# Attention scores on 64 array rows, rotary step with its half swap made by transfers, and a by-class copy of u, in a hybrid decoder block on one core

## The chip, the cores and the metric

The kernel runs on one core of one Trainium2 chip. The metric is device time in microseconds (us), as the median of several runs; a smaller number is better. Beside the timed runs, one execution was taken by the hardware profiler; all times of single instructions below come from that one execution.

## The reference, cut to what matters

One decoder layer on 512 tokens and 1024 features, all in float32: a SwiGLU feed-forward, a token-mixing part, a second feed-forward, a final norm. The change is nearly all in the token mixing. For normed and modulated tokens `u` it computes

```
proj = u @ w_in                      # pool p | q | k | v | gates
q, k = rope(q), rope(k)              # t1*cos - t2*sin , t2*cos + t1*sin  on the two 32-wide halves of a head
group 0: 4 heads, each query sees the last 128 keys
group 1: 4 heads, every 4th token; group 2: 4 heads, every 16th token
s = q k^T / 8, masked; softmax; o = p v       # head size 64
y_attn = sum over groups, weighted by their softmax denominators
y_pool = pooled p (windows 2, 4, 8, 16) through small matrices
out = (gate_p * (y_pool @ w_pb) + gate_a * (y_attn @ w_ab)) @ w_out
```

Groups 1 and 2 are computed on the four residue classes of the token number modulo 4 (class c holds the tokens 4i + c).

## The kernel before, in words

**Products.** Every float32 weight is split into two float32r parts (`whi`, `wlo`) and every activation likewise (`UH`, `UL` for u), and each product is three matmuls. TensorE runs these in an order written out by hand, nearly without a gap. Weights come in chunks of 512 KB into three buffers (`raw`); ScalarE makes `whi` (L298), VectorE makes `wlo` (L310) into a ring of seven chunks. `look`, `take`, `split` and `fetch` keep that pipeline some three chunks ahead of the matmuls. Each engine works its own program strictly in order; SyncE (queue SP) issues the transfers in program order as well.

**The mixing stage** (`mix`, L1173) goes so:

1. `head` makes q and k of group 0 in four banks, in the last 22 us before 381 us of the span.
2. `rope` (L974) turns two banks (first halves of four heads, second halves of four heads; `lay_mix` has ordered the columns so, by `qk_cols`) into `qt` or `kt`. Four VectorE products with cos and sin (L981), then two subtractions and two additions on 64 rows each (L987, L988). For groups 1 and 2 it also reorders the tokens by class, so that L987 and L988 read with a step of four elements.
3. The values of group 0 (L1222 to L1224), in four token blocks of 24 matmuls with 256 columns.
4. Eight tiles (`mm_tile`, L990; 24 matmuls with 512 columns each) make q and k of groups 1 and 2, and two more the pool inputs. Between their matmuls, hooks at given places k = 0..7 of a tile put the attention of group 0: one unit (token block n, pair of heads hp) per tile. A unit passes through `at_prep` (L1010: VectorE makes `qz`, a copy of q with the rows of the other head zeroed by the mask `hmask`), `at_scores` (L1022: fp32 matmuls with all 128 rows, then masking, maximum and exponentials), one tile later `at_turn` (L1062: transposes through TensorE, copy by ScalarE), and another tile later `at_values` (L1079).
5. `pool_diff` (L1140) works on GpSimd with the scratch tiles rt0 to rt2.
6. The values of groups 1 and 2 (L1272 to L1274): four classes c of 24 matmuls with 512 columns each. The stationary operand is `UH[k][:, c::4]` or `UL[k][:, c::4]`, read with a step of four elements. The units of groups 1 and 2, two per class, are hooked in here, their scores at k = 5 and k = 6.
7. Gates, merge and the output product follow.

**The second feed-forward** (`ffn2`, L787) makes the block sums for its saved products in a list of steps (`u_steps`, L673): additions on VectorE (L679, L695) and splits (L685 on ScalarE, then L686 on VectorE), put between the first tiles.

Of the kernel before, what the change touches and what calls it, by code (L numbers as in the profile page):

```python
# [14 lines left out]
P = 128  # L15
# [121 lines left out]
class Kernel:  # L137
# [535 lines left out]
    def u_steps(self, n):  # L673

        nc, v = self.nc, self.nc.vector
        (a11, a12), (a21, a22) = self.U4

        def add(o, x, y, op):
            return lambda: v.tensor_tensor(o, x, y, op=op)  # L679

        def split(i, u):
            def f():
                hi, lo = self.S[i]
                if i < 3:
                    nc.scalar.activation(hi, u, AF.Copy)  # L685
                    v.tensor_tensor(lo, u, hi, op=OP.subtract)  # L686
                    return
                nc.scalar.activation(hi, u.rearrange("p (k t) -> p k t", k=4), AF.Copy)
                v.tensor_tensor(lo, u.rearrange("p (k t) -> p k t", k=4), hi, op=OP.subtract)
            return f  # L690
# [96 lines left out]
    def ffn2(self):  # L787
        self.put, self.now = [], 0
        bk = [self.nb() for _ in range(4)]
        self.head(2, bk, AF.Silu)  # L790
        adds, (s2, s1, s0, last) = self.u_steps(2)
        self.todo = adds[:3] + [s0, adds[3], s2, adds[4], s1, adds[5]]
        do = lambda n: [self.todo.pop(0)() for _ in range(n)]
        for j in range(2):
            self.ffn_post(j, self.ffn_silu(j, bk[2 * j]), bk[2 * j + 1])
            do(2 + j)
# [4 lines left out]
        self.ffn(2, 4, last)  # L801
# [172 lines left out]
    def rope(self, pa, pb, dst, classes=1):  # L974

        v = self.nc.vector
        t = [self.rt.tile([P, 528], F32, name=f"rt{i}")[:, :T] for i in range(4)]
        for o, x, y in ((t[0], pa, self.cos), (t[1], pb, self.sin), (t[2], pb, self.cos), (t[3], pa, self.sin)):  # L980
            v.tensor_tensor(o, x, y, op=OP.mult)  # L981
        for half in (0, 1):
            rows = slice(64 * half, 64 * half + 64)
            cols = slice(T * half, T * half + T)
            src = [x[rows].rearrange("p (i c) -> p c i", c=classes) for x in t]
            to = [dst[r, cols].rearrange("p (c i) -> p c i", c=classes) for r in (slice(0, 64), slice(64, 128))]
            v.tensor_tensor(to[0], src[0], src[1], op=OP.subtract)  # L987
            v.tensor_tensor(to[1], src[2], src[3], op=OP.add)  # L988
# [21 lines left out]
    def at_prep(self, u):  # L1010

        kind, n, hp = u
        gs, toks = self.at_tokens(u)
        qz = self.aw.tile([P, T], F32, name="qz")
        for i, g in enumerate(gs):
            q = self.qt[g][:, hp * T:hp * T + T]
            for h in range(2):
                self.nc.vector.tensor_scalar(qz[:, (2 * i + h) * P:(2 * i + h + 1) * P], q[:, toks],
                                             self.hmask[:, h:h + 1], None, op0=OP.mult)
        self.qz[u] = qz  # L1020

    def at_scores(self, u):  # L1022
        kind, n, hp = u
        nc = self.nc
        M = nc.tensor.matmul
        self.si ^= 1
        S = self.bS[self.si]
        qz = self.qz.pop(u)
        gs, toks = self.at_tokens(u)
        for h in range(2):  # L1030
            o = h * 256
            if kind == 0:
                k = self.kt[0][:, hp * T:hp * T + T]
                if n == 0:
                    M(S[:, o + P:o + 2 * P], qz[:, h * P:h * P + P], k[:, 0:P], start=True, stop=True)
                else:
                    M(S[:, o:o + 2 * P], qz[:, h * P:h * P + P], k[:, (n - 1) * P:(n + 1) * P], start=True, stop=True)
            else:
                for i, g in enumerate(gs):
                    k = self.kt[g][:, hp * T:hp * T + T]  # L1040
                    M(S[:, o + i * P:o + i * P + P], qz[:, (2 * i + h) * P:(2 * i + h + 1) * P], k[:, toks],
                      start=True, stop=True)
# [8 lines left out]
        for h in range(2):  # L1051
            cs = slice(h * 256 + c0, h * 256 + 256)
            nc.vector.tensor_tensor_reduce(p[:, cs], S[:, cs], mask[:, c0:], 1.0, 3.0 * NEG, op0=OP.add, op1=OP.max,
# [25 lines left out]
    def at_values(self, u):  # L1079
# [14 lines left out]
        if kind == 0:  # L1094
            self.nc.vector.tensor_copy(self.o1[:, n, P * hp:P * hp + P], O)
        elif hp == 1:
            self.nc.vector.tensor_copy(self.o23[:, n, :256], self.bO[:, :256])
# [42 lines left out]
    def pool_diff(self, t, bank):  # L1140
# [3 lines left out]
        p, a, b = (self.rt.tile([P, 528], F32, name=f"rt{i}") for i in range(3))  # L1144
# [28 lines left out]
    def mix(self):  # L1173
        nc, tc = self.nc, self.tc
        v, M = nc.vector, nc.tensor.matmul
        self.prob, self.probT, self.pd, self.qz = {}, {}, {}, {}
        self.si = self.ti = 0
# [4 lines left out]
        with tc.tile_pool(name="ma", bufs=1) as ma, tc.tile_pool(name="rt", bufs=1) as self.rt, \  # L1182
                tc.tile_pool(name="aw", bufs=2) as self.aw, tc.tile_pool(name="stp", bufs=1) as self.stp:
# [17 lines left out]
            self.rope(bk[0], bk[1], self.qt[0])  # L1201
            self.rope(bk[2], bk[3], self.kt[0])
# [9 lines left out]
            for n in range(4):  # L1212
# [3 lines left out]
                if n == 3:  # L1216
                    self.at_prep((0, 0, 0))
# [7 lines left out]
                nc.scalar.activation(self.v1[:, n, :], b[:, :256], AF.Copy)  # L1225
            self.held = None
# [5 lines left out]
            def hooks(new, extra=(), nxt=()):  # L1232
# [6 lines left out]
                for i, u in enumerate(new):  # L1239
                    if u not in self.qz:  # L1240
                        h.setdefault(i, []).insert(0, lambda u=u: self.at_prep(u))
                    h.setdefault(5 + i, []).append(lambda u=u: self.at_scores(u))
                for u in nxt:
                    h.setdefault(6 + len(new) - 1, []).append(lambda u=u: self.at_prep(u))
# [14 lines left out]
            b = self.mm_tile(hooks([], nxt=g23[0]))  # L1259
            self.pool_diff(0, b)  # L1260
            b = self.mm_tile(hooks(g23[0], nxt=g23[1]))
# [3 lines left out]
            for c in range(4):  # L1265
                hk = hooks(g23[c + 1] if c < 3 else [])
                b = self.nb()
                for k in range(KT):
                    for f in hk.get(k, ()):
                        f()  # L1270
                    hi, lo = w[k]
                    M(b, self.UH[k][:, c::4], hi, start=k == 0, stop=False)  # L1272
                    M(b, self.UH[k][:, c::4], lo, start=False, stop=False)  # L1273
                    M(b, self.UL[k][:, c::4], hi, start=False, stop=k == KT - 1)  # L1274
# [73 lines left out]
    def build(self):  # L1348
# [24 lines left out]
        self.invf, self.hmask, self.icnt, self.ident = cst[:, 0:1], cst[:, 1:3], cst[:, 3:35], cst[:, 35:163]  # L1373
# [144 lines left out]
def constants():  # L1518
    i = np.arange(P)
    invf = (ROPE_THETA ** (-np.arange(0, HEAD_DIM, 2) / HEAD_DIM)).astype(np.float32)  # L1520
    hm = np.stack([(i % 64 // 32 == h) for h in range(2)], axis=1).astype(np.float32)
# [8 lines left out]
    return np.concatenate([invf[i % 32][:, None], hm, cnt, np.eye(P, dtype=np.float32),  # L1530
# [43 lines left out]
```

## Time and profile before

| what | value |
|---|---|
| time, median of 3 runs | 1013.88 us (1013.68 to 1016.19) |
| the profiled execution's own time | 1014.89 us |
| its span in the trace | 1013.1 us |
| TensorE busy | 1004.4 us, 99% of the span |
| VectorE busy | 763.9 us, 75% |
| ScalarE busy | 442.8 us, 44% |
| GpSimd busy | 26.9 us, 3% |
| mean granted TensorE clock | 0.999 |

The profiled execution's own time lies 1.8 us over its span: what is outside the first and the last instruction. A busy TensorE is one with a matmul somewhere in its pipe; one matmul of 512 columns is shown with some 0.39 us, while the next starts 0.23 us after it, so the pace has to be read from starts, not from durations. "PEld" is the loading of the stationary operand, which runs beside the matmul before.

### The profile page before, as it was taken

To read this page: it belongs to the slowest core of one execution; us is meant where nothing else is said; L and a number is where in the kernel's file an instruction comes from. 1 tells how busy PE (TensorE), PEld (TensorE's weight loads), DVE (VectorE), ACT (ScalarE), POOL (GpSimd) and SP (SyncE) were. 2 spreads that over 40 slices of the span, in tenths; PEclk is the share of its full clock that TensorE was granted. 3 is DMA by queue.
4 is the path that set the end of the run, shared out by engine and by line. 5 is a ranking of instruction groups with operands and counts; after the bars stand their busy time and mean duration, and the time that the engine had idled before them with its cause. 6 is when DMAs were issued, how large, how long until landed. Compare 5 with 4: busy or idle time off the path is not lost.

```text
span 1013.1 us, 15788 instructions
## 1 busy us (share of the span) xinstructions
PE 1004.4 (99%) x6460; PEld 912.8 (90%) x6460; DVE 763.9 (75%) x1117; ACT 442.8 (44%) x674; POOL 26.9 (3%) x31
## 2 busy tenths in 40 slices
PE   9999999999999999999999999999999999999997
PEld 7888999989899999889988888998899899998997
DVE  7989979789797677878447776577787776676754
ACT  6443644525435443334424323454365255352553
POOL 0000000000000000008000000000000000000002
PEclk9999999999999999999999999999999999999999
DMA  9755456455454323122155773412344234241312
GB/s 338 274 202 209 146 160 221 149 173 169 152 182 136 104 77 104 61 65 84 32 199 177 257 270 107 125 56 69 88 167 125 81 105 146 84 137 51 100 47 83
DMA packets 43146, 139.61 MB, mean 138 GB/s; under 512 B 4929, under 2 KB 8257, under 8 KB 43074
## 3 DMA queue, kind: packets, MB, share of 16 engines
q1 hardware_dynamic: 42498, 138.08, 41.4%
q8 instruction: 50, 0.82, 0.3%
q10 hardware_dynamic: 576, 0.52, 0.2%
q14 instruction: 22, 0.18, 0.0%
HBM read 135.82 MB, written 2.77 MB: 137 GB/s over the span
## 4 chain that ended last, share of the span: by engine, by line
PE 87%; DVE 7%; issue 2%; DMA 2%; ACT 1%; POOL 0%; SPq 0%; POOLq 0%; DVEq 0%; ACTq 0%
PE bank L342 15%; PE bank L343 15%; PE bank L341 15%; PE bank L719 10%; PE bank L721 10%; PE bank L720 10%; DVE wlo L310 2%; PE bank L1501 1%; PE bank L1503 1%; PE bank L1505 1%; PE bank L1093 1%; PE bank L1272 1%; DVE H L864 1%; PE bank L1273 1%; PE bank L1274 1%
## 5 line engine op out<-in xcount | busy, mean ns | idle before, releaser
L310 DVE TENSOR_TENSOR wlo<-raw,whi 128x1024 fp32r<-128x1024 f32 (+6 forms) x166 | 174.3, 1061 | 66.0 <-ACT whi L298 65.7
L298 ACT ACTIVATE whi<-raw 128x1024 fp32r<-128x1024 f32 (+6 forms) x166 | 149.9, 920 | 49.2 <-DVE raw L242 41.5
L719 PE MATMUL bank<-UH,whi 128*128 128x256 f32 x544 | 150.6, 277 | 0.2 <-ACT u L726 0.2
L721 PE MATMUL bank<-UH,wlo 128*128 128x256 f32 x544 | 150.5, 277 | 0.0
L720 PE MATMUL bank<-UL,whi 128*128 128x256 f32 x544 | 150.5, 277 | 0.0
L341 PE MATMUL bank<-HI,whi 128*128 128x512 f32 (+1 forms) x406 | 146.6, 361 | 0.0
L342 PE MATMUL bank<-HK,whi 128*128 128x512 f32 (+1 forms) x406 | 146.4, 361 | 0.0
L343 PE MATMUL bank<-HI,wlo 128*128 128x512 f32 (+1 forms) x406 | 146.2, 360 | 0.0
L341 PE MATMUL bank<-UH,whi 128*128 128x512 f32 (+1 forms) x400 | 145.9, 365 | 0.0
L343 PE MATMUL bank<-UH,wlo 128*128 128x512 f32 (+1 forms) x400 | 141.8, 355 | 0.5 <-DVE wlo L310 0.5
L342 PE MATMUL bank<-UL,whi 128*128 128x512 f32 (+1 forms) x400 | 141.8, 355 | 0.1
L310 DVE TENSOR_TENSOR wlo<-X,whi 128x1024 fp32r<-128x1024 f32 (+4 forms) x106 | 111.7, 1063 | 33.4 <-ACT whi L298 33.0
L298 ACT ACTIVATE whi<-X 128x1024 fp32r<-128x1024 f32 (+4 forms) x106 | 95.7, 926 | 47.8 <-DVE X L242 47.0
L719 PE MATMUL bank<-SH,whi 128*128 128x256 f32 x408 | 113.8, 279 | 0.1
L720 PE MATMUL bank<-SL,whi 128*128 128x256 f32 x408 | 113.6, 278 | 0.0
L721 PE MATMUL bank<-SH,wlo 128*128 128x256 f32 x408 | 113.6, 278 | 0.0
L719 PEld LDWEIGHTS bank<-UH,whi 128*128 128x128 f32 x544 | 102.1, 188 | 0.7 <-ACT u L726 0.4
L720 PEld LDWEIGHTS bank<-UL,whi 128*128 128x128 f32 x544 | 102.4, 188 | 0.3
L721 PEld LDWEIGHTS bank<-UH,wlo 128*128 128x128 f32 x544 | 102.1, 188 | 0.0
L342 PEld LDWEIGHTS bank<-HK,whi 128*128 128x128 f32 x406 | 76.3, 188 | 11.8 <-DVE HK L647 0.4
L341 PEld LDWEIGHTS bank<-HI,whi 128*128 128x128 f32 x406 | 76.5, 188 | 11.5
L343 PEld LDWEIGHTS bank<-HI,wlo 128*128 128x128 f32 x406 | 76.4, 188 | 11.6
(227 smaller groups left out, 1761.1 us busy)
## 6 DMA issues: line engine op xcount, KB each, us to landing
ada<-wada SPq DMA_DIRECT2D x47, 512.0 KB, 5.2
raw<-wmix SPq DMA_DIRECT2D x44, 512.0 KB, 3.7
raw<-wf1i SPq DMA_DIRECT2D x32, 512.0 KB, 4.3
raw<-wf2i SPq DMA_DIRECT2D x30, 512.0 KB, 3.5
X<-wf2i SPq DMA_DIRECT2D x14, 512.0 KB, 3.5
cs<-wada SPq DMA_DIRECT2D x12, 512.0 KB, 3.5
AR<-wada SPq DMA_DIRECT2D x12, 512.0 KB, 4.3
raw<-wf2o SPq DMA_DIRECT2D x12, 512.0 KB, 3.5
```

What stands on the lines that cost most here:

```text
L298: self.nc.scalar.activation(self.hi[:, y], r[:, x], AF.Copy)
L310: self.nc.vector.tensor_tensor(self.lo[:, y], r[:, x], self.hi[:, y], op=OP.subtract)
L341: M(ps, hi, uh, start=start, stop=False)
L342: M(ps, hi, ul, start=False, stop=False)
L343: M(ps, lo, uh, start=False, stop=stop)
L719: M(o, hi, uh, start=start and p == 0 and k == 0, stop=False, skip_group_check=True)
L720: M(o, hi, ul, start=False, stop=False, skip_group_check=True)
L721: M(o, lo, uh, start=False, stop=k == 3, skip_group_check=True)
L864: v.scalar_tensor_tensor(self.H[m + i], b, gate[:, m + i:m + i + 1], self.H[m + i], op0=OP.mult, op1=OP.add)
L1093: M(o, pt[:, blk * P:blk * P + P], v, start=i == 0, stop=i == len(srcs) - 1)
L1272: M(b, self.UH[k][:, c::4], hi, start=k == 0, stop=False)
L1273: M(b, self.UH[k][:, c::4], lo, start=False, stop=False)
```

## The change

Five things change.

1. **Layout of q and k.** A bank now holds two whole heads (64 rows each) and not four half heads; `qk_cols` is gone. `rope` becomes two steps. `rope_a`, right behind the bank: ScalarE copies the bank times +1 or -1 (`sign`) to a scratch tile, four transfers on SP swap the 32-row halves of it into a second tile `w`, and VectorE writes bank * cos into `dst`. `rope_b`, later: VectorE multiplies `w` by sin in place and adds it to `dst`. For group 0, `rope_b` stands between the blocks of its values; for the others at k = 6 of the next tile.
2. **Scores.** `at_prep`, `qz` and `hmask` are gone. The scores of head 0 use rows 0 to 63, those of head 1 rows 64 to 127, of `qt` and `kt` directly, each head into a bank of its own.
3. **Places.** The two units of a token block are hooked into one tile (both scores at k = 5, both `at_exp` behind them), the next tile has no new unit. In the class loop both units of a class have their scores at k = 5.
4. **By class.** `by_class` copies u's tokens 4i + c side by side (ScalarE, 16 copies of 128x512), half a class at a time into two buffers of each kind, and the matmuls of the values of groups 2 and 3 (in the code's count from 0: 1 and 2) take these as their stationary operand.
5. **Block sums.** In `ffn2` a split is put into the list as two steps, so that an addition of VectorE stands between ScalarE's copy and VectorE's subtraction.

The scratch tile rt0 becomes a part of `tr`. The copy of group 0's result out of its bank is made once for two units. The diff, cut:

```diff
-def qk_cols(base, g, second):
-    return np.concatenate([base + (4 * g + h) * 64 + 32 * second + np.arange(32) for h in range(4)])
...
-            for s in (0, 1):
-                ch.append(_fmajor(w_in, qk_cols(base, g, s)))
+            for hp in (0, 1):
+                ch.append(_fmajor(w_in, base + (4 * g + 2 * hp) * 64 + np.arange(P)))
...
+            x = u if i < 3 else u.rearrange("p (k t) -> p k t", k=4)
+            parts = [lambda: nc.scalar.activation(self.S[i][0], x, AF.Copy),
+                     lambda: v.tensor_tensor(self.S[i][1], x, self.S[i][0], op=OP.subtract)]
+            return parts if n else lambda: [f() for f in parts]
...
-        self.todo = adds[:3] + [s0, adds[3], s2, adds[4], s1, adds[5]]
+        self.todo = adds[:3] + [s0[0], adds[3], s0[1], s2[0], adds[4], s2[1], s1[0], adds[5], s1[1]]
...
-    def rope(self, pa, pb, dst, classes=1):
...
+    def rope_a(self, bank, dst, hp, classes, t, w):
+        nc = self.nc
+        nc.scalar.activation(t, bank, AF.Copy, scale=self.sign)
+        for i in range(4):
+            o = i ^ 1
+            nc.sync.dma_start(w[32 * o:32 * o + 32], t[32 * i:32 * i + 32])
+        by = lambda x: x.rearrange("p (i c) -> p c i", c=classes)
+        nc.vector.tensor_tensor(dst[:, hp * T:hp * T + T].rearrange("p (c i) -> p c i", c=classes), by(bank), by(self.cos),
+                                op=OP.mult)
+
+    def rope_b(self, dst, hp, classes, w):
         v = self.nc.vector
...
+        d = dst[:, hp * T:hp * T + T].rearrange("p (c i) -> p c i", c=classes)
+        v.tensor_tensor(w, w, self.sin, op=OP.mult)
+        v.tensor_tensor(d, d, w.rearrange("p (i c) -> p c i", c=classes), op=OP.add)
...
-    def at_prep(self, u):
...
     def at_scores(self, u):
...
+        for i, g in enumerate(gs):
+            for h in range(2):
+                rows = slice(64 * h, 64 * h + 64)
+                q, k = (x[g][rows, hp * T:hp * T + T] for x in (self.qt, self.kt))
+                if kind:
+                    o, ks = slice(i * P, i * P + P), toks
                 else:
...
+                    o, ks = (slice(0, 2 * P), slice((n - 1) * P, (n + 1) * P)) if n else (slice(P, 2 * P), toks)
+                S = self.bS[h][:, 2 * P * hp:2 * P * hp + 2 * P]
+                nc.tensor.matmul(S[:, o], q[:, toks], k[:, ks], start=True, stop=True, skip_group_check=True)
...
+            for i in range(4):
+                self.rope_a(bk[i], *to[i], 1, self.v23[:, i, :], sw[i])
...
+                for i in ((), (0, 1), (2,), (3,))[n]:
+                    self.rope_b(*to[i], 1, sw[i])
...
+                h.setdefault(5, []).extend(lambda f=f, u=u: f(u) for f in (self.at_scores, self.at_exp) for u in new)
...
-            todo = [[(0, n, hp)] for n in range(4) for hp in range(2)]
+            todo = [x for n in range(4) for x in ([(0, n, hp) for hp in range(2)], [])]
+            rest = []
             for g in (1, 2):
                 for dst in (self.qt[g], self.kt[g]):
-                    ps = [self.mm_tile(hooks(todo.pop(0), nxt=todo[0] if todo else ())) for s in range(2)]
-                    self.rope(ps[0], ps[1], dst, 4)
+                    for hp in range(2):
+                        b = self.mm_tile(hooks(todo.pop(0), rest))
+                        rt = [self.scratch(2 * i + hp)[:, :T] for i in range(2)]
+                        self.rope_a(b, dst, hp, 4, *rt)
...
+                        rest = [(6, lambda dst=dst, hp=hp, w=rt[1]: self.rope_b(dst, hp, 4, w))]
...
+            def by_class(i):
...
+                c, k = i // 2, i % 2 * 4
+                uc[i] = [self.uw.tile([P, T], F32R, name=n) for n in ("uch", "ucl")]
+                for o, x in zip(uc[i], (self.UHv, self.ULv)):
+                    nc.scalar.activation(o.rearrange("p (k i) -> p k i", k=4),
+                                         x.rearrange("p (k i c) -> p c k i", k=KT, c=4)[:, c, k:k + 4], AF.Copy)
...
+            b = self.mm_tile(hooks(g23[0], [(1, lambda: by_class(0)), (2, lambda: by_class(1))]))
...
-                    M(b, self.UH[k][:, c::4], hi, start=k == 0, stop=False)
-                    M(b, self.UH[k][:, c::4], lo, start=False, stop=False)
-                    M(b, self.UL[k][:, c::4], hi, start=False, stop=k == KT - 1)
+                    (hi, lo), (uh, ul) = w[k], (x[:, k % 4 * P:k % 4 * P + P] for x in uc[2 * c + k // 4])
+                    M(b, uh, hi, start=k == 0, stop=False)
+                    M(b, uh, lo, start=False, stop=False)
+                    M(b, ul, hi, start=False, stop=k == KT - 1)
+                    if k % 4 == 3 and c < 3:
+                        by_class(2 * c + 2 + k // 4)
```

More of the change, by code (lines that the diff above doesn't have):

```diff
@@ L800, in ffn2 @@
         self.ffn_pair(3)
-        self.ffn(2, 4, last)
+        self.ffn(2, 4, lambda: [f() for f in last])
     def open_ffn(self):
@@ L972, in trig_spread, with scratch @@
             self.nc.sync.dma_start(self.cs[32 * b:32 * b + 32], self.scr2)
-    def rope(self, pa, pb, dst, classes=1):
-        v = self.nc.vector
[L979 to L988, printed above, removed]
+    def scratch(self, i):
+        return self.rt.tile([P, 528], F32, name=f"rt{i}") if i else self.tr[:, :528]
+    def rope_a(self, bank, dst, hp, classes, t, w):
[8 more added lines that the diff above has]
+    def rope_b(self, dst, hp, classes, w):
+        v = self.nc.vector
+        d = dst[:, hp * T:hp * T + T].rearrange("p (c i) -> p c i", c=classes)
+        v.tensor_tensor(w, w, self.sin, op=OP.mult)
+        v.tensor_tensor(d, d, w.rearrange("p (i c) -> p c i", c=classes), op=OP.add)
     def mm_tile(self, hooks=()):
@@ L1024, in at_scores, with at_exp @@
         nc = self.nc
[L1025 to L1028, printed above, removed]
         gs, toks = self.at_tokens(u)
[L1030 to L1035, printed above, removed]
-                else:
[L1037 to L1042, printed above, removed]
+        for i, g in enumerate(gs):
[4 more added lines that the diff above has]
+                    o, ks = slice(i * P, i * P + P), toks
+                else:
+                    o, ks = (slice(0, 2 * P), slice((n - 1) * P, (n + 1) * P)) if n else (slice(P, 2 * P), toks)
+                S = self.bS[h][:, 2 * P * hp:2 * P * hp + 2 * P]
+                nc.tensor.matmul(S[:, o], q[:, toks], k[:, ks], start=True, stop=True, skip_group_check=True)
+    def at_exp(self, u):
+        kind, n, hp = u
+        nc = self.nc
         p = self.aw.tile([P, T], F32, name="prob")
@@ L1143, in pool_diff @@
         w0 = POOL_W[2 * t]
-        p, a, b = (self.rt.tile([P, 528], F32, name=f"rt{i}") for i in range(3))
+        p, a, b = (self.scratch(i) for i in range(3))
         d = self.kt[0][:, T * t:T * t + T]
@@ L1175, in mix @@
         v, M = nc.vector, nc.tensor.matmul
-        self.prob, self.probT, self.pd, self.qz = {}, {}, {}, {}
-        self.si = self.ti = 0
+        self.prob, self.probT, self.pd = {}, {}, {}
+        self.ti = 0
         outer = ExitStack()
@@ L1520, in constants @@
     invf = (ROPE_THETA ** (-np.arange(0, HEAD_DIM, 2) / HEAD_DIM)).astype(np.float32)
-    hm = np.stack([(i % 64 // 32 == h) for h in range(2)], axis=1).astype(np.float32)
+    sign = np.where(i % 64 < 32, 1, -1).astype(np.float32)
     cnt = np.zeros((P, 32), np.float32)
```

56 lines of the change are left out of this document (15 added, 41 removed).

## The prediction

> **What bounds the kernel now.** I read the page's busy times first, then the waits of TensorE, then the stretches of the mixing stage.
>
> ```profile
> span 1013.1 us, 15788 instructions
> PE 1004.4 (99%) x6460; PEld 912.8 (90%) x6460; DVE 763.9 (75%) x1117; ACT 442.8 (44%) x674; POOL 26.9 (3%) x31
> ```
>
> TensorE has work in it for all but 8.7 us. So an edit pays only if it takes matmul time away, quickens the pace, or ends one of TensorE's few waits. Its waits, first for 380 to 531 us of the span, then for 660 to 720 us, are one each:
>
> ```profile
> PE bank L1070 <- ACT prob L1058: 0.2, 1, 0.2
> PE bank L343 <- DVE wlo L310: 0.5, 1, 0.5
> ```
>
> 0.7 us in all. Then the windows, with the columns PE, PEld, DVE, ACT, POOL: everything from the first tile behind group 0's values to the last values of the classes, and the class loop alone.
>
> ```profile
> 393.10:504.50 111.40, 111.10 (x599) 98.72 (x598) 79.27 (x193) 42.09 (x103) 21.56 (x20) 1.00 0.25 79
> 466.20:504.50 38.30, 38.30 (x226) 37.50 (x226) 21.35 (x65) 18.03 (x46) 14.46 (x14) 1.00 0.17 53
> ```
>
> Granted clock 1.00; VectorE and ScalarE have room. The edit must shorten these 111.4 us. All its savings are TensorE's.
>
> **By-class copies.** Starts in TensorE's timeline give the pace: twelve matmuls of the class loop, then twelve plain ones.
>
> ```profile
> 474.24 0.40 PE L1272 MATMUL bank<-whi,UH 128*128 128x512 f32 x1
> ...
> 476.82 0.39 PE L1274 MATMUL bank<-whi,UL 128*128 128x512 f32 x1
> ...
> 504.46 0.40 PE L341 MATMUL bank<-UH,whi 128*128 128x512 f32 x1
> ...
> 506.96 0.39 PE L343 MATMUL bank<-UH,wlo 128*128 128x512 f32 x1
> ```
>
> Eleven steps take 2.58 us (0.2345 each) with the operand read in steps of four, 2.50 us (0.2273) without. 96 matmuls: 0.69 us. The loads say why:
>
> ```profile
> L1272 PEld LDWEIGHTS bank<-whi,UH x32: 307/309/311, 465.9 to 503.5; 128*128 128x128 f32 x32
> L1222 PEld LDWEIGHTS bank<-whi,UH x32: 188/192/192, 381.5 to 392.6; 128*128 128x128 f32 x32
> ```
>
> A stepped load lasts 0.31 us against 0.19. Small matmuls put between cannot cover it. Scores in a plain tile, then in the loop:
>
> ```profile
> 463.87 1.05 PE L1041 MATMUL bank<-k,qz 128*128 128x128 f32 x8
> 464.68 0.48 PE L341 MATMUL bank<-UH,whi 128*128 128x512 f32 x1
> 465.00 0.39 PE L342 MATMUL bank<-UL,whi 128*128 128x512 f32 x1
> ...
> 470.80 1.05 PE L1041 MATMUL bank<-k,qz 128*128 128x128 f32 x8
> 471.61 0.60 PE L1272 MATMUL bank<-whi,UH 128*128 128x512 f32 x1
> 472.05 0.40 PE L1273 MATMUL bank<-wlo,UH 128*128 128x512 f32 x1
> ```
>
> The first big matmul behind an interruption takes 0.32 us (0.093 over pace) in a plain tile and 0.44 (0.205 over) in the loop. The loop has 14 interruptions (4, 4, 4, 2 by class); with both scores at k = 5 it has 11 (3, 3, 3, 2). 14 x 0.205 - 11 x 0.093 = 1.85 us. Together **2.5 us**.
>
> **Fewer places.** In the eight tiles and the first pool tile group 0 has 24 interruptions (scores, turn, values, each 8); two units at a time leave 4 + 8 + 4. The second pool tile goes from two to one. 9 x 0.093 = **0.8 us**.
>
> **Scores on half the rows.** From the chain of waits, four records of 256 columns, four of 128, and sixteen of the 64-column values as a measure for loads:
>
> ```profile
> 417.39 0.86 PE bank L1037 x4
> 396.68 0.45 PE bank L1035 x4
> 478.48 1.73 PE bank L1093 x16
> ```
>
> A 256-column record takes 0.215 us. Eight of 128 columns took 0.81 (463.87 to 464.68), 0.101 each. The values have half those columns and still need 1.73 / 16 = 0.108: at 128 columns and below it is the load that sets the pace. The number of score matmuls stays at 48 of two records each. If head 0 on rows 0 to 63 and head 1 on rows 64 to 127 run side by side, a block of eight 256-column records (three such blocks) shrinks from 1.72 us to five steps of 0.215, since a matmul's own two records follow each other: 0.65 us saved, three times 2.0. For 128 columns I take nothing, as halving the rows need not shorten a load. Bounds: nothing at all where halves do not overlap; where the loads overlap too, the four class blocks go from 16 steps to 9 (7 x 0.101 x 4 = 2.8) and the first block from 8 to 5 (0.3), 5.1 in all. I take **2.0**, the value that the rows bear without a new assumption on loads.
>
> The trace shows no change between whole-array and half-array matmuls. There will be 8 blocks, 16 edges. Nearest rows: changing to transposes or fp32 scores costs the 0.093 counted above. From above, a pipe that empties: 0.40 shown less 0.227 pace is 0.17, with an uncovered load of 0.19 it is 0.36: 0 to 5.8 us. I take 0, the interruption row being the nearest.
>
> The Trainium skill, page "TensorEngine Tiling (Array Packing)", section "Key Properties", speaks against this: a change of tiling mode, though not of the tile, drains TensorE. No row here shows such a change; by that rule, with 0.17 an edge, the sum would lose 2.7 us. The same section says that different tiles can run loads and matmuls in parallel, which would be the 5.1 us. I weigh both as rivals.
>
> **The two waits.** The 0.2 us stood behind a long rope on VectorE, which is split now. The 0.5 us is in the second feed-forward:
>
> ```profile
> 694.88 1.22 DVE L686 TENSOR_TENSOR SL<-X,SH 128x1024 fp32r<-128x1024 f32 x1 [1.19 <-ACT SH L685]
> 696.02 1.22 DVE L679 TENSOR_TENSOR X<-X 128x1024 f32<-128x1024 f32 x1
> 697.15 2.35 DVE L310 TENSOR_TENSOR wlo<-raw,whi 128x1024 fp32r<-128x1024 f32 x2
> ```
>
> The addition now fills the 1.19 us of waiting, and L686 goes behind `wlo`, which starts some 2.3 us earlier than 697.15, more than the 0.5 that TensorE waited. Two more sums each move an addition into such a gap; nothing is added. **0.7 us.**
>
> **What the rotary step adds, and what hides it.** TensorE never waits for it if it lands in time. The tightest place is the first scores:
>
> ```profile
> 384.99 1.05 ACT L298 ACTIVATE whi<-raw 128x1024 fp32r<-128x1024 f32 x1
> ...
> 390.69 1.14 ACT L298 ACTIVATE whi<-raw 128x256 fp32r<-128x256 f32 x2
> 391.15 3.57 DVE L310 TENSOR_TENSOR wlo<-raw,whi 128x1024 fp32r<-128x1024 f32 x4
> 396.52 0.60 PE L1035 MATMUL bank<-k,qz 128*128 128x128 f32 x4
> L972 SPq DMA_DIRECT2D cs<-scr x4: 408/422/426, 321.4 to 322.8; - x4
> DMA to landing us min/median/max: 3.8/3.9/4.1
> L1147 ACT ACTIVATE rt<-bank 128x512 f32<-128x512 f32 x2 | 1.2, 598 | 4.8 <-PE bank L343 3.7 <-POOL k L1162 1.1
> ```
>
> ScalarE copies four banks from about 380.5 on (0.6 each, to 383). SP issues 16 transfers at 0.42 (the nearest row, also 32 rows), 381.2 to 387.9; they land 3.9 later, the last at 391.8. VectorE's four products with cos end at 383.5; behind them stands the first `wlo` (386 to 387.2), the sine parts of both q banks (1.4 each, to 390.0), a `wlo` (391.2), a k bank (392.6), two `wlo` pieces (393.9), the last k bank (395.3). The scores come at 396.5: **1.2 us of room**. Past that, each us later is a us of TensorE. The queues behind fare better than before: `wlo` began only at 391.15, and the raw buffers with it.
>
> For groups 1 and 2, VectorE's rows:
>
> ```profile
> 390.43 0.69 DVE L988 TENSOR_TENSOR k<-rt,rt 64x512 f32<-64x512 f32 x1
> 404.33 0.69 DVE L981 TENSOR_TENSOR rt<-bank,cs 128x512 f32<-128x512 f32 x1
> ...
> 410.46 1.08 DVE L988 TENSOR_TENSOR q<-rt,rt 64x512 f32<-64x512 f32 x1
> ```
>
> A stepped operation costs 1.08 against 0.69. Per bank: 1.08 (cos) + 0.69 (sine) + 1.08 (sum) = 2.85, two banks 5.7, against 4 x 0.69 + 4 x 1.08 = 7.1 in one piece before, and no `qz`. VectorE gains. The wait that comes in: the sine product for its transfer, with the next bank's product and `wlo` queued behind. A bank's copy is done some 2 us behind its tile (four exponentials are ahead on ScalarE), four issues 1.7, landing 3.9: about 7.6, where the product's place is some 4.6 into the next tile. So VectorE may stand 3 us, plus 1.8 of work. Before, one rope held `wlo` back from 404.33 to 411.54, 7.2 us, and TensorE waited only the 0.2 quoted above: that cover holds. On SP the weight loads queue behind four transfers that wait for ScalarE, some 4 us, under the same cover. 32 transfers here take SP 13 us of some 70.
>
> ScalarE gets 12 signed copies (0.6) and 16 class copies, each 0.6 like L1147, or 0.94 if a step of four costs it the 1.08 / 0.69 of VectorE: 9.6 to 15 us more on 18.03 in a stretch of about 35. Hidden. A class copy waits for the matmuls of the class before to release its buffer, with softmax copies and `whi` behind it; its users come half a class later, about 4 us. GpSimd's work only changes buffers.
>
> **Sum:** 2.5 + 0.8 + 2.0 + 0.7 = 6.0 us. The execution with this span took 1014.89 us, 1.8 over its span; 6.0 less gives a span of 1007.1 and 1008.9 us for it. The median shown is 1013.88, 1.0 lower: **1007.9 us**.
>
> **Rivals.**
> 1. The loads of the halves overlap as well: 3.1 us more, 1004.8 us. For it: the loads set the pace at 128 columns. Against: no row shows two loads at once. This is what the skill's "in parallel" would give. 0.17.
> 2. Every edge of a score block empties the pipe: 2.7 to 5.8 us given back, 1010.6 to 1013.7. For it: 0.17 of depth is there in each matmul; against: other changes of kind cost 0.093. This is the skill's drain. 0.18.
> 3. Slower: the halves don't overlap and the pipe empties at each change of half: 40 changes inside the blocks and 16 edges, 56 x 0.17 = 9.5 us, less the 4.0 of the other terms: 5.5 us slower, 1019.4. It turns slower beyond 4.0 / 56 = 0.07 us a change. Against: the rows loaded for one half are not those in use by the other. 0.10.
> 4. A wait takes their place: the swaps land late. 3 us beyond the room give 1010.9; a loss needs 6.0. For it: 16 transfers at once with a single row to price them; against: the DMA share is 0.25 and SP idle. The change then shifts work and shows little of what it says. 0.10.
>
> The forecast keeps 0.45 (own range 1006 to 1009.5). **Range** 1003.7 to 1012.5: rival 1 and most of 2 and 4 in, rival 3 and the tails (0.2) out. A measurement of this kernel tells about 0.3% (3.0 us) from no change. Faster than 1010.8: 0.45 + 0.17 + 0.06 (rival 2) + 0.04 (rival 4) = 0.72; slower than 1016.9: 0.10 + 0.02 = 0.12; between: 0.16.
>
> **What would show it.** The class loop's load at 0.19 and its pace at 0.227; 11 interruptions of 0.32 there. A 256-column score block near 1.1 us, a class block near 1.6 (0.9 by rival 1). More than 0.45 us from the last half-row matmul to the second big one: rival 2. TensorE's waits: none near 698, none at the first scores. From the first tile to the last class matmul 111.4 should come to about 106. What would make it wrong: a wait of TensorE on `q` or `k` near 396, or on a class copy.

## The result and the profile after

The changed kernel took 1012.94 us (1010.9 to 1014.75, 22 runs), the kernel before on the same chips 1014.5 us (1013.38 to 1016.19, 22 runs): ratio 0.9984, 95% interval 0.9978 to 0.999. So it is faster by 1.6 us, inside the 0.3% that the prediction called no difference. 6.0 us had been forecast.

The page of the changed kernel (its profiled execution took 1012.59 us):

```profile
span 1010.8 us, 15868 instructions
PE 1000.0 (99%) x6460; PEld 901.9 (89%) x6460; DVE 742.0 (73%) x1053; ACT 465.6 (46%) x702; POOL 26.5 (3%) x31
```

TensorE is busy for 4.4 us less, but idle for 10.8 us where it was 8.7. Its waits between 340 and 540 us are one, and it is new:

```profile
PE bank L1055 <- ACT prob L1043: 2.6, 1, 2.6
```

The windows, with the columns PE, PEld, DVE, ACT, POOL, clock, DMA share and GB/s: the tiles up to the first class matmul, the class loop up to the first gate matmul, and two stretches behind the wait.

```profile
392.90:463.20 70.30, 70.30 (x374) 57.26 (x373) 46.38 (x92) 33.06 (x71) 5.66 (x6) 1.00 0.42 128
463.20:503.20 40.00, 37.21 (x225) 30.38 (x224) 14.27 (x42) 29.58 (x57) 15.54 (x15) 0.96 0.15 47
475.80:480.60 4.80, 4.74 (x23) 4.22 (x24) 0.73 (x2) 4.11 (x10) 4.20 (x4) 0.64 0.23 89
480.60:485.00 4.40, 4.40 (x34) 3.53 (x34) 1.40 (x2) 3.39 (x4) 0.00 (x0) 1.00 0.01 2
```

Before, the same two parts took 73.1 us (393.1 to 466.2) and 38.3 us. The tiles gained 2.8 us where 3.0 had been forecast; the class loop, which should have gained 2.5 us, lost 1.7 us. For 4.8 us behind its wait TensorE was granted 0.64 of its clock. Its timeline there (start, duration, what it does):

```profile
472.78 0.39 PE L1271 MATMUL bank<-whi,ucl 128*128 128x512 f32 x1
475.81 1.15 PE L1055 MATMUL bank<-cst,prob 128*128 128x128 f32 x4 [2.65 <-ACT prob L1043]
476.61 0.78 PE L1269 MATMUL bank<-whi,uch 128*128 128x512 f32 x1
477.18 0.63 PE L1270 MATMUL bank<-wlo,uch 128*128 128x512 f32 x1
478.04 2.73 PE L1078 MATMUL bank<-v,probT 128*128 128x64 f32 x16
480.61 0.61 PE L1055 MATMUL bank<-cst,prob 128*128 128x128 f32 x4
```

The transposes take 0.80 us to the next start where they take 0.36 elsewhere, the values 2.57 where they take 1.73. The values show the clock alone; part of the 0.80 us is still waiting, for the exponentials of the second head (in e1 below, the same late transposes took 0.69 us at a granted clock of 1.00). What made the exponentials late stands in the timeline of ScalarE, GpSimd and VectorE in the 12 us ahead:

```profile
464.54 0.19 ACT L1043 ACTIVATION_READ_ACCUMULATOR prob<-prob,negmax 128x1 f32 x1
465.45 1.28 POOL L1145 TENSOR_TENSOR k<-k,tr 64x512 f32<-64x512 f32 x1
466.76 0.60 ACT L1130 ACTIVATE tr<-bank 128x512 f32<-128x512 f32 x1 [2.03 <-POOL k L1145]
467.25 1.05 ACT L294 ACTIVATE whi<-raw 128x1024 fp32r<-128x1024 f32 x1
...
468.68 1.14 ACT L1255 ACTIVATE uch<-UH 128x512 fp32r<-128x512 f32 x1
...
469.71 1.12 ACT L1255 ACTIVATE ucl<-UL 128x512 fp32r<-128x512 f32 x1
...
471.22 1.05 ACT L294 ACTIVATE whi<-raw 128x1024 fp32r<-128x1024 f32 x1
472.30 1.88 DVE L306 TENSOR_TENSOR wlo<-raw,whi 128x1024 fp32r<-128x1024 f32 x1 [2.64 <-ACT whi L294]
474.09 0.41 DVE L1038 CUSTOM_DVE_ANT_0 prob<-bank,masks 128x256 f32<-128x256 f32 x1
...
475.15 0.51 ACT L1043 ACTIVATE prob<-prob,negmax 128x256 f32<-128x256 f32 x1 [2.89 <-DVE negmax L1040]
```

Read it as one chain over three engines. ScalarE is done with the softmax of class 0 at 464.7 and comes to the copy of the second pool tile into `tr`. GpSimd still reads the first pool tile from that buffer, so ScalarE stands for 2.03 us. Behind it, in program order, come `whi`, two class copies of some 1.1 us and the next `whi`. VectorE's `wlo` needs that `whi`, the masking and the maximum (L1038) stand behind `wlo`, and the exponentials need the maximum. They come 2.65 us too late for TensorE. Before, ScalarE had a shorter wait at the same place, and TensorE had no wait behind it:

```profile
468.45 0.60 ACT L1147 ACTIVATE rt<-bank 128x512 f32<-128x512 f32 x1 [1.09 <-POOL k L1162]
```

### The profile page after: what moved, and what is told of

Its sections match the earlier page's. It is cut to its first block, busy times and chain, and to the rows that moved or that the text cites. A ratio compares the mean times of both kernels' runs of the same rounds, so it can differ in the third digit from the quotient of the medians.

```text
span 1010.8 us, 15868 instructions
## 1 busy us (share of the span) xinstructions
PE 1000.0 (99%) x6460; PEld 901.9 (89%) x6460; DVE 742.0 (73%) x1053; ACT 465.6 (46%) x702; POOL 26.5 (3%) x31
## 4 chain that ended last, share of the span: by engine, by line
PE 90%; DVE 3%; DMA 2%; issue 1%; ACT 1%; POOL 1%; SPq 0%; POOLq 0%; DVEq 0%; ACTq 0%
PE bank L337 17%; PE bank L338 17%; PE bank L339 17%; PE bank L710 10%; PE bank L712 10%; PE bank L711 10%; PE bank L1500 1%; PE bank L1502 1%; PE bank L1504 1%; PE bank L1078 1%; DVE wlo L306 1%; DMA ada<-wada 1%; PE bank L1055 1%; DMA H<-xT 1%; DMA AR<-wada 1%
```

## The experiments

The theory after the first look: the class copies on ScalarE and its wait for GpSimd push the exponentials behind TensorE's need, and the standing TensorE then loses its clock. Rivals: the copies alone, ScalarE's load as a whole, or the place of the weight split. "Class loop" is the time from its first matmul to the first gate matmul (38.3 us before, 40.0 after).

| kernel | median us | ratio to before (95%) | class loop us |
|---|---|---|---|
| changed | 1012.94 | 0.9984 (0.9978 to 0.999) | 40.0 |
| e1 pool tile of its own | 1009.99 | 0.9956 (0.9943 to 0.9968) | 37.5 |
| e2 stepped reads, no copies | 1009.28 | 0.9949 (0.9936 to 0.9961) | 36.7 |
| e3 low parts on VectorE | 1012.56 | 0.997 (0.996 to 0.998) | 40.6 |
| e4 = e1 + e3 | 1008.39 | 0.994 (0.9927 to 0.9952) | 35.9 |
| e5 = e4, split later | 1013.31 | 0.9984 (0.9975 to 0.9993) | 42.6 |
| e6 = changed, split later | 1011.21 | 0.9967 (0.9955 to 0.998) | 38.3 |
| e7 = e2, half by half | 1011.88 | 0.9971 (0.996 to 0.9982) | 38.2 |
| e8 = e4, old block sums | 1009.75 | 0.995 (0.9936 to 0.9963) | 35.9 |
| e9 = e2, one half only | 1015.57 | 1.0009 (0.9999 to 1.0018) | 39.2 |
| e11 = e4, split at k = 1 | 1007.73 | 0.9935 (0.9922 to 0.9948) | 35.8 |
| e12 = e4, split at k = 2 | 1008.54 | 0.9943 (0.9929 to 0.9957) | 35.8 |
| e13 = e1, split at k = 1 | 1008.02 | 0.9931 (0.9917 to 0.9944) | 34.6 |

### What makes the wait: e1 to e4

e1, a scratch tile of its own for the second pool input, so that ScalarE needn't wait for GpSimd:

```diff
-        p, a, b = (self.scratch(i) for i in range(3))
+        p, a, b = (self.scratch(i) for i in ((0, 1, 2), (3, 1, 2))[t])
```

> The changed kernel, but the second pool input is copied to a scratch tile of its own (rt3), so ScalarE does not wait for GpSimd's last reading of the first one. Theory A (ScalarE's program stands still behind that copy, so the exponentials of class 1 are late, TensorE waits 2.65 us for them and then runs some us at a lower clock): the copy starts some 2.0 us earlier, the wait of 2.65 us shrinks to about 0.6 or goes, the granted clock stays at 1.00 in the class loop, and the time falls by about 4.5 us, to about 1008.5 (ratio to the kernel before about 0.994). Rival B (the wait only takes up slack that would be waited for a class later; the gain of the half-row scores is lost at their edges): the time falls by at most 1 us.

e2, no copies by class; the matmuls read u in steps of four again:

```diff
-            b = self.mm_tile(hooks(g23[0], [(1, lambda: by_class(0)), (2, lambda: by_class(1))]))
+            b = self.mm_tile(hooks(g23[0]))
...
-                    (hi, lo), (uh, ul) = w[k], (x[:, k % 4 * P:k % 4 * P + P] for x in uc[2 * c + k // 4])
+                    (hi, lo), uh, ul = w[k], self.UH[k][:, c::4], self.UL[k][:, c::4]
...
-                    if k % 4 == 3 and c < 3:
-                        by_class(2 * c + 2 + k // 4)
```

> The changed kernel without the class copies: the values of groups 1 and 2 read u with a step of four again. Theory A: ScalarE's chain is 2.2 us shorter ahead of the late exponentials, and the class loop itself slower, so the wait of 2.65 us goes with the loss of clock (4.5 us won), and the 2.5 us of stepped loads come back: about 2 us below the changed kernel, 1010.9 (ratio about 0.996). Rival C (the class copies gain nothing at all, they only load ScalarE): as fast as the run with the tile of its own, about 1008.5 or less.

e3, the copies of `ucl` on VectorE:

```diff
-                    nc.scalar.activation(o.rearrange("p (k i) -> p k i", k=4), ..., AF.Copy)
+                    (lambda: nc.scalar.activation(o, x, AF.Copy), lambda: v.tensor_copy(o, x))[j]()
```

> The changed kernel, with the copies of the low part (ucl) on VectorE instead of ScalarE; ScalarE still waits for GpSimd. Theory A: only one class copy (1.11 us) stands ahead of the late exponentials instead of two, the wait falls from 2.65 to about 1.6 us, and the time by 1 to 3 us, to 1010 to 1012 (how much of the loss of clock goes with it is not foreseen). Rival B: no change.

e4, e1 and e3 together:

> Both: the second pool input in a tile of its own and the low copies on VectorE. Theory A: no wait left in the class loop, 1008.0 (ratio 0.9935), no more than 0.6 us below the run with the tile alone. Rival B: within 1 us of the changed kernel.

TensorE's waits in e1 and in e4 (total, times, longest):

```profile
PE bank L1055 <- ACT prob L1043: 1.4, 2, 1.0
```

```profile
PE bank L1055 <- ACT prob L1043: 0.3, 1, 0.3
PE bank L1078 <- DVE v L1277: 0.2, 1, 0.2
```

In e2 there is none, though ScalarE waits for GpSimd as long as in the changed kernel:

```profile
467.47 0.60 ACT L1130 ACTIVATE tr<-bank 128x512 f32<-128x512 f32 x1 [2.04 <-POOL k L1145]
```

So each cause alone is borne or nearly so (2.04 us of GpSimd without copies: no wait; copies without GpSimd: 1.0 us at most), and only both together make the 2.65 us. (Some 0.5 us may be a third part: the `wlo` ahead of the maximum took 1.88 us, where it took 1.39 in the kernel before and in e2. GpSimd was at work beside all three, and no run tries that by itself.) Taking either away gives 3 to 4 us back. e3 left the wait at 1.8 us, and a clock of 0.70 in the 5 us from 475: copies moved to VectorE stand in front of the same `wlo` and maximum.

```profile
PE bank L1055 <- ACT prob L1043: 1.8, 1, 1.8
```

Whether the copies pay depends on what is left of the wait. In e1, with them, the class loop is 0.8 us longer than in e2 without them; in e4 it is 0.8 us shorter, though the intervals of e4's and e2's times overlap. Of the four forecasts only e4's time came out (1008.0 forecast, 1008.39 measured): e1 was 1.5 us slower than forecast, since 1.4 us of waiting was left, e2 1.6 us faster, and e3 lies above its 1010 to 1012.

### Where the weight split stands: e5, e6, e11, e12, e13

e5 and e6 move the class loop's weight split behind the exponentials:

```diff
-                    if k == 4:
+                    if k == 5:
```

> The run with the pool tile of its own and the low copies on VectorE, and the weight split of the class loop put behind the exponentials (at k = 5, behind the hooks, where it was at k = 4), so that ScalarE and VectorE make the softmax of a class ahead of the next weight chunk. Theory A (it is the order on ScalarE and VectorE that makes the probabilities late): the remaining 0.75 us of TensorE's standing in the class loop goes, 1007.6. Rival: the weight chunk is late instead and TensorE waits for wlo: the same time or more.

> The changed kernel with nothing but the weight split of the class loop put behind the exponentials. ScalarE still waits 2.0 us for GpSimd. Theory A: the exponentials of class 1 no longer stand behind a whi of ScalarE (1.05) and a wlo of VectorE (1.9), so they start some 3 us earlier, the wait of 2.65 us is gone or under 0.5, the clock stays at 1.00, and the time is 1008.5, at most 1009.5. Rival B (GpSimd's hold alone makes the wait): still over 1.5 us of wait and 1011 or more.

Both forecasts missed. The wait for the exponentials went in both, but another took its place, in e5 first and then in e6:

```profile
PE bank L1078 <- DVE v L1277: 4.0, 3, 2.1
```

```profile
PE bank L1078 <- DVE v L1277: 2.6, 3, 1.8
```

Now `whi` is behind the exponentials, `wlo` behind `whi`, and behind `wlo` on VectorE the copy of the values' bank that the next matmuls read. The rivals for e5 had named `wlo` itself; it was the instruction behind it. So e11 and e12 moved the split the other way, to k = 1 and k = 2 of e4, and e13 to k = 1 of e1, with all sixteen copies left on ScalarE:

> The best version so far (pool difference in a scratch tile of its own, low parts of the class copies on VectorE) with the weight split of the class loop three steps earlier, at k = 1 instead of k = 4. Left in that version are two waits of TensorE, 0.3 us for the exponentials and 0.2 us for the copy of the values' bank. Theory A (whatever stands in front of the exponentials on ScalarE and of the maximum on VectorE sets those waits): with the split three steps (2.0 us) earlier whi and wlo are done before the masking starts; both waits go, 0.5 us less, some 1007.9. Theory B (in the first class the split is bound by its weight's landing or by a free buffer, so that earlier in the program it holds up what stands behind it, the copy of probabilities on ScalarE and the second half's class copy): new waits on probT or on the class copies, 1009 or more.

> As the run with the split at k = 1, but at k = 2, behind the copies that k = 1 and k = 2 put on ScalarE for the values. Theory A: both waits go as well, some 1007.9. Theory B: between the best version (1008.4) and the run with k = 1.

> The changed kernel with the pool difference in a scratch tile of its own and the weight split of the class loop at k = 1; all sixteen class copies stay on ScalarE. Theory A (what was wrong is the order in which ScalarE and VectorE reach the maximum and the exponentials, not ScalarE's load): the two waits for the exponentials (1.4 us in the run with the scratch tile alone) go, since both halves of wlo are done before the masking; class loop 35.2 us, time as the best version, 1007.7 to 1008.5. Theory B (ScalarE with copies of 1.1 us is itself too full in the 9.4 us of a class: exponentials 1.9, copies of probabilities 1.2, class copies 4.4, whi 1.05, all that at about 8.6): the second class copies or the copies of probabilities come late in each class, waits return, 1009.5 or more.

In e11 and e12 the wait for the exponentials is gone, but two of 0.2 us are left, both for VectorE: one for the copy of the values' bank, one for a `ucl` copy itself. In e11:

```profile
PE bank L1078 <- DVE v L1277: 0.2, 1, 0.2
PE bank L1271 <- DVE ucl L1256: 0.2, 1, 0.2
```

So e11 came to its 1007.9 (1007.73) although only one of the two waits went, and e12 (1008.54) to neither of its forecasts. In e13 TensorE doesn't wait at all between 340 and 540 us, and its class loop is the shortest of all. Its windows (tiles, then class loop) and, from its VectorE's and ScalarE's timeline, the split that now comes ahead of the maximum:

```profile
393.90:464.20 70.30, 70.30 (x375) 57.18 (x374) 46.35 (x92) 33.11 (x71) 5.69 (x6) 1.00 0.41 127
464.20:498.80 34.60, 34.60 (x225) 29.19 (x224) 15.63 (x42) 29.85 (x57) 16.23 (x15) 1.00 0.17 54
```

```profile
467.17 3.65 DVE L306 TENSOR_TENSOR wlo<-raw,whi 128x1024 fp32r<-128x1024 f32 x2 [2.59 <-ACT whi L294]
470.73 0.41 DVE L1038 CUSTOM_DVE_ANT_0 prob<-bank,masks 128x256 f32<-128x256 f32 x1
...
471.85 0.51 ACT L1043 ACTIVATE prob<-prob,negmax 128x256 f32<-128x256 f32 x1 [0.74 <-DVE negmax L1040]
```

The masking starts at 470.73 and the exponentials at 471.85 with ScalarE idle before them: 7.7 us behind the start of the class loop, where the changed kernel needs 12.0 and e1, which differs from e13 in the place of the split alone, 10.2 (473.81 from 463.62). ScalarE is as busy as in the changed kernel (29.85 us against 29.58). That tells order from load: ScalarE had the time, the program asked for it in the wrong sequence. e13, e11 and e4 have intervals that overlap; which is the fastest stays open, that each beats both kernels does not.

### Two halves of the array side by side: e7, e9

e7 is e2 with both units' head 0 first and then both units' head 1:

```diff
-            for h in range(2):
+            for h in (half,):
...
-                h.setdefault(5, []).extend(lambda f=f, u=u: f(u) for f in (self.at_scores, self.at_exp) for u in new)
+                h.setdefault(5, []).extend(lambda u=u, x=x: self.at_scores(u, x) for x in range(2) for u in new)
+                h.setdefault(5, []).extend(lambda u=u: self.at_exp(u) for u in new)
```

> The run without class copies (1009.3, no wait of TensorE in the mixing stage), with the scores of both units made for head 0 first and then for head 1, so that neighbours use the same half of the rows. Theory S (the blocks are short because neighbours on different halves run side by side): a block of eight 256-column records goes from 1.07 to 1.5 or 1.6 us, a class block of sixteen 128-column records from 1.09 to 1.5 or 1.6, together some 3.3 us: about 1012.6. Rival L (they are short because a load or a pass over 64 rows is shorter by itself): the blocks stay as they are, 1009.3.

e9 is e2 with the scores of both heads on rows 0 to 63:

```diff
-                rows = slice(64 * h, 64 * h + 64)
+                rows = slice(0, 64)
```

> The kernel with stepped reads (no class copies), in which both heads' scores are read from rows 0 to 63. The scores of head 1 are left out: those of head 0 are computed twice. The order is head by head alternating, as in the changed kernel. So no two neighbouring matmuls can use different rows. Open from the half-by-half run: its class blocks (128 columns) went from 1.09 to 1.64 us, but its three blocks of 256 columns stayed at 1.07. Theory A (everything that was saved is side-by-side work of the two halves, and in the half-by-half order the 256-column blocks still overlapped across their two pairs): the 256-column blocks go back to 1.7 us, the class blocks to 1.6; time 3 x 0.65 + 4 x 0.55 = 4.2 us over the kernel with stepped reads, some 1013.4. Theory B (a 64-row pass of 256 columns is shorter by itself, only the 128-column blocks work side by side): 256-column blocks 1.07 again, class blocks 1.6, time 2.2 us over it, some 1011.5.

TensorE's timelines: the changed kernel, alternating halves; then e7; then e9. In each a block of eight 256-column records and one of sixteen 128-column records, each with the next matmul's start.

```profile
408.72 0.48 PE L337 MATMUL bank<-UH,whi 128*128 128x512 f32 x1
409.04 0.39 PE L338 MATMUL bank<-UL,whi 128*128 128x512 f32 x1
409.26 0.40 PE L339 MATMUL bank<-UH,wlo 128*128 128x512 f32 x1
409.59 1.14 PE L1022 MATMUL bank<-k,q 64*128 64x256 f32 x8
410.66 0.51 PE L337 MATMUL bank<-UH,whi 128*128 128x512 f32 x1
411.00 0.40 PE L338 MATMUL bank<-UL,whi 128*128 128x512 f32 x1
...
467.62 1.16 PE L1022 MATMUL bank<-k,q 64*128 64x128 f32 x16
468.71 0.50 PE L1269 MATMUL bank<-whi,uch 128*128 128x512 f32 x1
```

```profile
410.14 1.14 PE L1022 MATMUL bank<-k,q 64*128 64x256 f32 x8
411.22 0.50 PE L337 MATMUL bank<-UH,whi 128*128 128x512 f32 x1
...
469.07 1.71 PE L1022 MATMUL bank<-k,q 64*128 64x128 f32 x16
470.71 0.62 PE L1270 MATMUL bank<-whi,UH 128*128 128x512 f32 x1
```

```profile
409.20 1.99 PE L1022 MATMUL bank<-k,q 64*128 64x256 f32 x8
411.12 0.50 PE L337 MATMUL bank<-UH,whi 128*128 128x512 f32 x1
...
470.89 2.05 PE L1022 MATMUL bank<-k,q 64*128 64x128 f32 x16
472.86 0.62 PE L1269 MATMUL bank<-whi,UH 128*128 128x512 f32 x1
```

With all scores on one half the blocks need 1.92 and 1.97 us, alternating 1.07 and 1.09. e9's time is 6.3 us over e2's; three blocks of 0.85, four of 0.88 and the first block (1.09 against 0.65) are 6.5. So the short blocks come from the two halves working at once, for 128 columns too. That a 64-row pass is shorter by itself is out. (The forecast had 1.7 and 1.6 us for the blocks and 4.2 us in all: right in kind, too small in size. e7's had both kinds of block grow, and only the 128-column ones did.) In e7 the 128-column block lost 0.55 us of its 0.88 and the 256-column block nothing. If some three records of the second half may start before the first half is done, both fit (3.5 records of 0.24 saved there, 2.7 of 0.12 here); that is worked out, not shown.

### The block sums: e8

e8 is e4 with the sums of the second feed-forward in the old order:

```diff
-        self.todo = adds[:3] + [s0[0], adds[3], s0[1], s2[0], adds[4], s2[1], s1[0], adds[5], s1[1]]
+        self.todo = adds[:3] + [lambda: [f() for f in s0], adds[3], lambda: [f() for f in s2], adds[4], lambda: [f() for f in s1], adds[5]]
```

> The run with the pool tile of its own and the low copies on VectorE, with the block sums of the second feed-forward in their order before the change. If the new order is worth its 0.5 us: TensorE waits 0.5 us for wlo near 693 us again, time 1008.9 against 1008.4. If something else was late there anyway: no wait, or no difference in the stretch from 680 to 715.

The wait near 698 us is back, and in e4 it was not there:

```profile
PE bank L339 <- DVE wlo L306: 0.5, 1, 0.5
```

The median is 1.4 us over e4's, the span of the profiled execution 0.2 us (1007.7 against 1007.5), and the two intervals overlap. So half a microsecond is below what these times resolve, and the evidence is the row.

## Why the prediction was wrong, point by point

**The step that failed: "Hidden."** The prediction costed the ScalarE copies by their sum against ScalarE's room in the stretch (9.6 to 15 us more on 18.03 in 35) and said of GpSimd that its work "only changes buffers". In place of a hidden copy the runs show a wait of TensorE of 2.65 us and 4.8 us at 0.64 of its clock behind it. The price was low: a class copy took 1.11 us, so sixteen take 17.8, where 15 was the upper bound. The room was there all the same: ScalarE had 29.85 us to do in e13's class loop of 34.6, and TensorE didn't wait. But an in-order engine has to be on time at each instruction, and the prediction named what is queued behind a class copy (softmax copies and `whi`) without following `whi` on to `wlo`, the maximum and the exponentials. Nor did it ask what happens to the wait for GpSimd where the tiles end earlier, though the row of L1147 that it quotes for a copy's price has 1.1 us of that wait in it. Both kernels use one buffer for both pool tiles (rt0, now `tr`). GpSimd came free 1.7 us earlier (466.73 against 468.42), ScalarE's last exponential ended 2.6 us earlier (464.73 against 467.36), so the wait grew from 1.09 to 2.03 us. e1 and e2 each take one of the two causes away; e13 shows that, with the buffer of its own, the order was enough to mend the rest.

**What it cost.** From the starts in TensorE's timelines of the changed kernel and of e13, 5.4 us of class loop: 2.8 us of standing, 1.9 us in the 5 us behind it (the low clock, and at most some 0.3 us for the second head's exponentials, by e1's 0.69 against 0.36), 0.5 us of late exponentials again two classes later, 0.1 us for a `wlo`. In time, 1012.94 less 1008.02 is 4.9 us.

**The terms of the sum held.** The class loop of e13 is 3.7 us shorter than before. The copies' 2.5 and three blocks at 0.53 less 0.12 make 3.7. Neither e2 nor e13 has a wait of TensorE, so the difference of their class loops should be the copies: 2.0 us (36.69 to 34.65), where 0.69 + 11 x 0.112 was 1.9. The tiles gained 2.8 us against 0.8 + 2.0 + 0.2, partly by luck: the two bounds below nearly cancel in them (some 0.6 us each way). From the first tile to the last class matmul e13 needs 104.9 us, the changed kernel 110.3; some 106 was forecast. The 256-column blocks are at 1.07 us, as forecast. The 0.5 us near 698 went (e8).

**Two bounds were taken wrongly, in opposite directions.** For the 128-column blocks the prediction took nothing, since halving rows need not shorten a load: 1.09 us for sixteen records, where two blocks of 0.81 stood before, is 0.53 us each, 2.1 in all (rival 1's bound was 2.8). The Trainium skill, page "TensorEngine Tiling (Array Packing)", section "Key Properties", has tiles load and multiply in parallel; e9 agrees, 1.97 us against 1.09. For the edges it took nothing either: going into a block takes 0.33 us from the start before (409.26 to 409.59) where 0.23 is the pace, coming out 0.34 where other interruptions have 0.32. That is 0.12 a block, 1 us for eight. The same section of the Trainium skill has a change of tiling mode drain TensorE; if these edges are that drain, it costs here a fifth or less of the 5.8 us that rival 2 allowed. Some of the edge may lie inside the 1.09 us as well. The prediction's own sign for rival 2, more than 0.45 us from the last half-row matmul to the second big one, is met: 0.55 us (468.50 to 469.05), where the whole-array block before had 0.35 (464.65 to 465.00). That may be why the block missed rival 1's 0.9; no run separates the two. Counted by blocks, from 1.09 and 0.12, the sum is 7.1; e13 measured 6.7 (1014.69 to 1008.02).

**The rotary step** was hidden, as said: no wait at the first scores. That its room was near the forecast (the last k bank is done at 394.70, the scores start at 396.42: 1.7 us, where 1.2 was forecast) is in part luck, as two prices were off in opposite directions. An issue of a transfer between scratch tiles took 0.62 us (eight in 4.98, from SP's timeline of the changed kernel), for which 0.42 was taken; the landing took 2.0 us, for which 3.9 was taken.

```profile
381.30 4.98 SPq L976 DMA_DIRECT2D q<-v  x8
```

**Rivals.** Rival 1 was three quarters true (2.1 of 2.8 us for the class blocks), rival 2's drain there but small outside the blocks (1 us), rival 3's halves in sequence are out (e9). The one that decided was of rival 4's kind, a new wait in the place of the old, but not in its place: on a copy's followers and not on a transfer. The last line of the prediction had named "a class copy" as what would make it wrong; TensorE waited not for the copy but for what stood behind it.

## What to carry to other kernels

Room on an engine over a stretch doesn't hide an instruction that is put into an in-order queue: follow the first instruction behind it that another engine needs, and on from there, until TensorE. When TensorE's part gets shorter, look for buffers whose readers don't get shorter with it; a wait of 1 us grew to 2 here, which was harmless without the new copies behind it (e2) and not with them. Where a new wait appears, try the order (an earlier split) and the buffer first: neither gave an engine more work, and together they brought 4.9 us back, while moving copies to another engine left waits of its own.

## What the runs showed of the hardware

- **A short standstill of TensorE can lower its clock.** In the profiled executions, waits of 2.65 us (changed kernel), 2.08 (e5) and 1.84 (e3) were followed by some 5 to 9 us at a mean granted clock of 0.54 to 0.64; a wait of 1.83 us (e6) and waits up to 1.1 (e1, e5) were not. In e5:

```profile
478.00:483.00 5.00, 5.00 (x28) 4.25 (x29) 0.42 (x1) 1.92 (x3) 1.83 (x3) 0.50 0.00 0
```

  Measured from the wait's end to the same instruction in a run without the drop, the low clock cost up to 1.9 us in the changed kernel (against e13), 3.2 in e5 (against e6) and 3.2 in e3 (against e1): about as much as the wait or more. The Trainium skill, page "TensorE: Matmul & The Clock Gate", section "Part 1: The HAM clock gate", puts the drop to half clock behind at least one idle window of about 3.4 us; here it came behind shorter waits. The length of the wait alone doesn't decide, with 1.83 and 1.84 us on either side. Nor does the program: of e3's eleven timed executions seven had a mean clock of 0.995 or 0.996 and took 1012.39 to 1013.62 us, four had 0.998 to 1.000 and took 1009.42 to 1011.1. So e3's median depends on how often the drop came. What decides wasn't tried.
- **A stepped read costs ScalarE nearly double:** a class copy of 128x512 takes 1.11 us, a plain one 0.60 from a bank and 0.63 from another tile (`whi` of 128x512). VectorE's copy of the same takes 0.62 us, and 1.47 (e11) to 1.50 (e4) while GpSimd makes its additions (L1136). `wlo` took 1.88 us beside GpSimd in the changed kernel instead of 1.22; in the kernel before it took 1.39 beside the same additions, so no fixed price follows.
- **Two 64-row halves** with records in turn run at 0.068 us a record of 128 columns, one half alone at 0.123.
